# Three edits to a three-layer hybrid network on one core: SSD exponents on ScalarE, conditioning of the first layer by TensorE, gates stored as rows

## The chip, the cores and the metric

The kernel runs on one core of a Trainium2 chip. A core has five engines that run side by side, each with its own in-order instruction stream: TensorE (PE, with weight loads shown apart as PEld), VectorE (DVE), ScalarE (ACT), GpSimd (POOL) and SyncE (SP), which here issues every DMA. The metric is device time in microseconds, the median over several runs.

## The reference, cut to what matters

One block of a first kind (gated linear attention and a bidirectional SSD, both in chunks) is followed by two layers of a second kind. Every layer is conditioned: a vector c gives shifts, scales and gates. What the change touches is the conditioning and the SSD's decay between two tokens of a chunk.

```python
ada = jax.nn.silu(c)[:, None, :] @ w_ada[layer] + b_ada[layer]      # 1024 -> 6 x 1024
sh1, sc1, g1, sh2, sc2, g2 = jnp.split(ada, 6, axis=-1)
...
cum = jnp.cumsum(ai, axis=1)                                        # one SSD chunk of 128 tokens
seg = cum[:, :, None] - cum[:, None, :]
Lm = jnp.exp(jnp.where(mask, seg, -jnp.inf))
cb = jnp.einsum('btgn,bsgn->btsg', ci, bi)
y = jnp.einsum('btsg,btsge,bsgep->btgep', cb, Lm, xi)
y = y + jnp.einsum('btgn,bgenp->btgep', ci, S) * jnp.exp(cum)[..., None]
...
h_lat = h_lat + g1 * mix
h_lat = h_lat + g2 * _swiglu(modulate(rms_norm(h_lat, norm2_w[layer]), sh2, sc2), ...)
...
mod = cond @ w_ada[l] + b_ada[l]                                    # each of the two later layers
```

The sequence has 512 tokens and a context of 256, the model width is 1024. The SSD has 4 groups of 8 heads of width 64, in 4 chunks of 128 tokens, forward and backward.

## The kernel before, in words

Weights come in tiles of 128 x 1024 fp32. `feed` loads one (`wr`), ScalarE rounds it to a high part (`wh`), and DVE or POOL takes the rest (`wl`), so that each product is made of three fp32r matmuls (`mm3`). There are three buffers of each kind, so PE can run some tiles ahead of a late load, and no further.

The program is written as stages: start, `gla` (linear attention), `ssd`, the merge and the first layer's feed-forward, and then two layers of the second kind. A scheduler orders each engine's instructions by its own estimate of the times, with buffers and semaphores as limits, so neighbouring stages overlap. All DMAs are on SP's queue: one that waits for a free buffer holds back all that stand behind it.

In the `ssd` stage each group g goes through `ssd_dense` (the projections of B, C and x with a convolution, transposes through the PSUM bank `dtr`, of which there is one), `ssd_z` (a gate) and `ssd_scan`. For each chunk and each half of the heads, `ssd_scan` reads two broadcast rows of summed decays, `rf` and `rb` (three buffers each, 258 KB), takes from them the per-token columns of `TM` (one instruction on DVE, one on POOL), joins both by a predicated copy, takes the exponent on ScalarE and multiplies by `cb`. The result stands as weights before x on PE. At the end of a chunk, `a1` is divided by its norm (`ss`) on DVE, transposed and spilled to `sp_ob`.

Conditioning runs beside this, in 8 steps that `more(n)` pulls from `conditions()`: two for each of g1, sh2, sc2, g2 of the first layer. The later layers' vectors are pulled within the feed-forward stages. `cond_col` computes one vector: for each half of 512 columns it loads eight 128 x 512 pieces of the weight (`cw`), ScalarE scales each by an element of silu(c) per partition, POOL adds it to `cacc`; the sum is split into three bf16 parts (`rsc`, `qx`), and PE sums these over the partitions by products with one column of ones, twelve for each half. `to_row` then turns a gate into a row: the 128 x 8 tile is written to memory element by element (`rg1-1d`, `rg2-1d`, and `rg10d` to `rg21d` in the later layers), and read back much later as a row broadcast to all partitions (`row`).

The first two vectors (sh1, sc1) are made in the start stage in another way: the weight is a moving operand of 512 columns, silu(c) a stationary operand of 32 columns (`cs`), and four products fill the four strips of PE at once.

Of the kernel before, what the change touches and what calls it, by code (L numbers as in the profile page):

```python
# [7 lines left out]
F32 = mybir.dt.float32  # L8
# [37 lines left out]
def _col(v):  # L46

    return np.asarray(v).reshape(-1, P).T
# [19 lines left out]
def prep(x):  # L68
# [15 lines left out]
    w_ada = g["w_ada"][0]  # L84

    A["wa1"] = np.ascontiguousarray(w_ada[:, :2048].reshape(2, 4, P, 2, 4, 256).transpose(4, 0, 2, 1, 3, 5).reshape(4, 2, P, 2048))
    A["wa"] = np.ascontiguousarray(w_ada[:, 2048:])
    A["ba"] = np.ascontiguousarray(g["b_ada"][0][None, 2048:])
    lr = np.concatenate([cols("dtf"), cols("dtb"), cols("lrf"), cols("lrb"), np.zeros((D, 32), np.float32)], 1)
    A["w_lr"] = _feat(lr)[0]  # L90
    A["w_qk"] = np.stack([_feat(np.concatenate([cols("q", 128 * h, 128 * h + 128), cols("k", 128 * h, 128 * h + 128)], 1))
# [22 lines left out]
    pk = _Pack()  # L114
    c2 = np.stack([_col(g["c"][0]), _col(g["c_ctx"])], 2)
    pk.add("c2", c2.reshape(P, 16))
    ba = _col(g["b_ada"][0][:2048])
    pk.add("ba_sh", ba[:, :8])
    pk.add("ba_sc", ba[:, 8:])
    pk.add("gnw", _col(g["gla_norm_w"][0]))  # L120
    pk.add("snw", _col(g["ssm_norm_w"][0]))
    pk.add("n1w", _col(g["norm1_w"][0]))
# [91 lines left out]
def build(tc, I, out, at, dbg=None, stop=None):  # L214
# [71 lines left out]
    def PS(tag="sm"):  # L286
        return new(banks[-1].pool, [P, 512], F32, tag, banks[-1].tags[tag])
# [10 lines left out]
    def tt(o, a, b, op, e=V):  # L298
        note(o, e.tensor_tensor(o, a, b, op=op))  # L299

    def ts(o, a, s1, s2, op0, op1=None, e=V):
        if op1 is None:
            note(o, e.tensor_scalar(o, a, s1, None, op0=op0))  # L303
        else:
            note(o, e.tensor_scalar(o, a, s1, s2, op0=op0, op1=op1))
# [7 lines left out]
    def load(o, i):  # L313
        return note(o, nc.sync.dma_start(o, i))
# [110 lines left out]

    qp = es.enter_context(tc.tile_pool(name="qp", bufs=1))

    def cond_col(src, bias, cc, k0, plus, tag):

        r = qp.tile([P, NK], F32, name=tag)  # L430
        sums = []
        prev = recent[0]

        def late(i):
            tc.add_manual_dep(i.ins, prev, nosync, reason="not before")

        for j in range(2):
            acc = W("cacc", NC[0])
            late(memset(acc, 0.0))
            load(acc[0:1], bias[:, k0 + 512 * j:k0 + 512 * j + 512])  # L440
            for k in range(NK):
                w = W("cw", NC[1])
                late(load(w, src[k * P:(k + 1) * P, k0 + 512 * j:k0 + 512 * j + 512]))
                copy(w, w, scale=cc[k])
                tt(acc, acc, w, A_, e=G)

            s2, s3 = T([P, 2, 512], "rsc", 1, BF), T([P, 512], "qx", 1, BF)
            for i in range(2):
                copy(s2[:, i], acc)
                tt(s3 if i else acc, acc, s2[:, i], S_, e=G)  # L450
            sums.append([s2[:, 0], s2[:, 1], s3])
        yield None
        for j in range(2):
            p = PS("dtr" if "dtr" in banks[-1].tags else "o2")
            for k in range(4):
                for i, a in enumerate(sums[j]):
                    mm(p[:, k:k + 1], a[:, k * P:(k + 1) * P], ones_b[:, 0:1], i == 0, i == 2)
            ts(r[:, 4 * j:4 * j + 4], p[:, :4], plus, None, A_)
        yield r

    def silu_cols(src, tag):
        c1, th = qp.tile([P, NK], F32, name=tag), qp.tile([P, NK], F32, name=tag + "t")
# [4 lines left out]

    def to_row(c, scale, name):

        t = qp.tile([P, NK], F32, name=name)  # L470
        ts(t, c, scale, None, M_)
        d = dp.tile([NK, P], F32, name=name + "d")
        load(d.rearrange("k p -> p k"), t)
        return d.rearrange("k p -> (k p)")[None, :].to_broadcast([P, D])

    def row(d, tag, bufs=1):
# [7 lines left out]
        o, w = at[2][n]  # L484
        return Cl[l][:, o + a:o + (w if b is None else b)]

    cc = silu_cols(col("c2").rearrange("p (k j) -> p k j", j=2)[:, :, 0], "cc1")

    def conditions():

        for l, src, bias, n0, gs in ((-1, I["wa"], I["ba"], 2, 0.5), (0, I["w2a0"], I["b2a0"], 0, 1.0),
                                     (1, I["w2a1"], I["b2a1"], 0, 1.0)):
            for i, n in list(enumerate(("sh1", "sc1", "g1", "sh2", "sc2", "g2")))[n0:]:
                for r in cond_col(src, bias, cc if l < 0 else cc2, 1024 * (i - n0), 1.0 if n[:2] == "sc" else 0.0,
                                  f"m{n}{l}"):
                    if r is not None:
                        mod[l, n] = to_row(r, gs, f"r{n}{l}") if n[0] == "g" else r
                    yield

    mod = {}  # L500
    parts = conditions()
    NC = [2, 2]

    def more(n):
        for _ in range(n):
# [12 lines left out]
        t = T([P, S], "act", 25, F32R, ap)  # L518
        hC.append([t[:, :CTX], t[:, CTX:]])
    with phase("start"):  # L520
        cs = T([P, NK, 32], "cs")
        memset(cs, 0.0)
        th = T([P, 16], "th")
        act(th, col("c2"), AF.Tanh, scale=0.5)
# [330 lines left out]
    def ssd_steps():  # L855
# [4 lines left out]
        for n, o, nch in ((S, 0, 4), (CTX, S, 2)):  # L860
# [32 lines left out]
            if nch == 4:  # L893
                ts(Q, d3, 1e-37, None, OP.max)
                act(Q, Q, AF.Ln)
                tt(X[0:32], X[0:32], Q[0:32], S_)
                tt(X[32:64], X[32:64], Q[32:64], A_)
                copy(it[0:32], E1[0:32])
                copy(it[32:64], E2[32:64])
# [156 lines left out]
    def ssd_scan(g, d):  # L1056
# [24 lines left out]
        for c in range(4):  # L1081
# [3 lines left out]
            for hf in range(2):  # L1085
# [3 lines left out]
                for r_, rw in ((rf, fr), (rb, br)):  # L1089
                    load(r_, sp_A[rw, c * 129:(c + 1) * 129][None].to_broadcast([P, 4, 129]))  # L1090
                e1, e2 = rf[:, :, 1:129], rb[:, :, 0:128]
                tt(e1, e1, TM[:, c, 0, fr][:, :, None].to_broadcast([P, 4, P]), S_)
                tt(e2, TM[:, c, 0, br][:, :, None].to_broadcast([P, 4, P]), e2, S_, e=G)
                V.copy_predicated(e1, before, e2)
                act(e1, e1, AF.Exp)
                tt(e1, e1, cb[:, sl][:, None, :].to_broadcast([P, 4, P]), M_)
# [22 lines left out]
            act(sq, a1, AF.Square, acc=ss)  # L1119
            ts(ss, ss, 1.0 / 512, 4 * EPS, M_, A_)  # L1120
            rsq(ss)
            ts(a1, a1, ss, None, M_)
            ons.append(a1)
        for i in range(4):
            pt = PS()
# [4 lines left out]
    with phase("ssd"):  # L1130
# [8 lines left out]
            ssd_z(g, d)  # L1139
            ssd_scan(g, d)  # L1140
        more(8 - sum(MS))
        NC[:] = 2, 4
        for j in range(NG + NH, NK):
            gate_tile(I["w_gb"][j], sp_gb[j])
        oa = load_T(sp_oa)
# [766 lines left out]
```

## Time and profile before

| | |
|---|---|
| median of 3 runs | 2895.77 us (2894.13 to 2898.12) |
| profiled execution | 2891.66 us, of this the span 2889.7 us |
| granted TensorE clock, mean | 0.978 |
| PE, DVE, ACT, POOL busy | 94%, 64%, 46%, 40% of the span |
| conditioning weights, first layer (`cw<-in_wa`) | 64 DMAs of 256 KB |
| conditioning weights, later layers (`cw<-in_w2a`) | 192 DMAs of 256 KB |

Durations are of one profiled execution; the time of a run has some two microseconds outside its span. Matmuls overlap, so the sum of their durations is over the time they take; a pitch, from start to start, is the better number. A row of groups ends in the engine's idle time before them and what ended it. "Clock" is the share of TensorE's full clock that was granted in a window.

### The profile page before, as it was taken

Reading aid. Unit: us, or ns where it says so; the run is one execution under the profiler, and the core shown is the slowest. Engines: PE = TensorE matmul, PEld = TensorE weight load, DVE = VectorE, ACT = ScalarE, POOL = GpSimd, SP = SyncE. Lnnn points to the kernel's source line nnn. Section 1 sums busy time; section 2 is a strip of 40 time slices with the busy share of each in tenths; the row PEclk is TensorE's granted clock in tenths of the full one; section 3 lists DMA queues with packets and bytes.
Section 4 is the critical chain, followed back from the end, with each engine's and each line's share of the span. In section 5 each row is a group of like instructions: output and inputs, shape, how many; then the busy total and the mean of one; then the engine's idle time right before and its main releaser. Section 6 shows DMA issues by size and latency. Waiting matters only on the chain. (4 is left out here: it accounts for less than half of the span.)

```text
span 2889.7 us, 40511 instructions
## 1 busy us (share of the span) xinstructions
PE 2702.3 (94%) x15230; PEld 2215.4 (77%) x15230; DVE 1858.2 (64%) x2844; ACT 1328.7 (46%) x2307; POOL 1158.2 (40%) x790
## 2 busy tenths in 40 slices
PE   7999999988989899999999999999998999999997
PEld 5898988777776678777877877777777887788886
DVE  4777756968877475434555557764767655765457
ACT  5533334335343335634346654653634664443232
POOL 2333304536556144846631235574654123600013
PEclk9999999999999999999999999999999999999999
DMA  6222224444456754655422112655532220332222
GB/s 242 74 77 74 81 89 139 110 97 132 131 151 202 230 176 151 192 146 165 138 90 90 63 41 81 198 163 150 185 118 81 78 73 24 100 105 93 93 94 78
DMA packets 160308, 346.31 MB, mean 120 GB/s; under 512 B 20848, under 2 KB 55920, under 8 KB 159088
## 3 DMA queue, kind: packets, MB, share of 16 engines
q1 hardware_dynamic: 160112, 343.72, 38.6%
q8 instruction: 120, 1.97, 0.3%
q14 instruction: 76, 0.62, 0.1%
HBM read 326.73 MB, written 16.94 MB: 119 GB/s over the span
## 5 line engine op out<-in xcount | busy, mean ns | idle before, releaser
L311 PE MATMUL acc<-act,wh 128*128 128x512 f32 (+1 forms) x2944 | 877.5, 383 | 34.8 <-DVE act L299 16.9
L299 DVE TENSOR_TENSOR wl<-wr,wh 128x1024 fp32r<-128x1024 f32 (+1 forms) x329 | 466.9, 1421 | 442.6 <-ACT wh L296 441.8
L311 PEld LDWEIGHTS acc<-act,wh 128*128 128x128 f32 x2944 | 533.5, 193 | 161.0 <-DVE act L299 25.4
L296 ACT ACTIVATE wh<-wr 128x1024 fp32r<-128x1024 f32 (+1 forms) x344 | 358.9, 1045 | 510.2 <-PE sm L311 202.3
L311 PE MATMUL acc<-act,wl 128*128 128x512 f32 (+1 forms) x1472 | 530.6, 378 | 0.6 <-DVE wl L299 0.5
L311 PE MATMUL acc<-wh,act 128*128 128x256 f32 (+2 forms) x2312 | 499.7, 303 | 10.0 <-ACT cacc L290 7.1
L299 POOL TENSOR_TENSOR cacc<-cacc,cw 128x512 f32<-128x512 f32 x256 | 402.6, 1574 | 220.6 <-DMA cacc<-in_b2a_dram 86.4
L311 PEld LDWEIGHTS acc<-wh,act 128*128 128x128 f32 x2312 | 378.4, 190 | 31.2 <-ACT cacc L290 8.3
L311 PE MATMUL sm<-act,wh 128*128 128x512 f32 (+1 forms) x1232 | 376.2, 382 | 0.0
L311 PE MATMUL acc<-wl,act 128*128 128x256 f32 (+2 forms) x1156 | 350.5, 303 | 0.8 <-POOL wl L299 0.8
L311 PEld LDWEIGHTS acc<-act,wl 128*128 128x128 f32 x1472 | 273.0, 192 | 56.1 <-issue 8.2
L296 ACT ACTIVATE cw<-cw,cc 128x512 f32<-128x512 f32 x256 | 181.4, 721 | 262.0 <-DMA cw<-in_w2a_dram 155.3
L311 PEld LDWEIGHTS sm<-act,wh 128*128 128x128 f32 x1232 | 228.4, 189 | 46.3
L311 PE MATMUL sm<-act,wl 128*128 128x512 f32 (+1 forms) x616 | 235.0, 381 | 1.2 <-DVE wl L299 1.2
L311 PEld LDWEIGHTS acc<-wl,act 128*128 128x128 f32 x1156 | 220.0, 190 | 10.6 <-issue 1.9
L299 POOL TENSOR_TENSOR wl<-wr,wh 128x1024 fp32r<-128x1024 f32 x52 | 138.1, 2658 | 200.2 <-DVE wh L303 123.1
L299 POOL TENSOR_TENSOR wr<-wr,row 128x1024 f32<-128x1024 f32 x42 | 107.5, 2565 | 185.8 <-DMA f<-sp_yb 69.9
L299 POOL TENSOR_TENSOR x<-x,gx 128x512 f32<-128x512 f32 x32 | 49.4, 1570 | 300.0 <-DVE gx L299 300.0
L299 POOL TENSOR_TENSOR act<-act,wgt 128x128 f32<-128x128 f32 (+3 forms) x64 | 50.1, 801 | 246.3 <-DVE wgt L299 173.9
L311 PEld LDWEIGHTS sm<-act,wl 128*128 128x128 f32 x616 | 116.1, 189 | 25.7 <-DVE wl L299 2.5
L311 PE MATMUL sm<-wh,act 128*128 128x512 f32 (+1 forms) x392 | 124.2, 378 | 0.0
L1668 DVE CUSTOM_DVE_ANT_0 sm<-sm,K 128x128 f32<-128x128 f32 (+3 forms) x128 | 63.2, 497 | 86.1 <-PE sm L311 81.1
(440 smaller groups left out, 4626.1 us busy)
## 6 DMA issues: line engine op xcount, KB each, us to landing
cw<-in_w2a_dram SPq DMA_DIRECT2D x192, 256.0 KB
wr<-in_w2u_dram SPq DMA_DIRECT2D x88, 512.0 KB
wr<-in_w2d_dram SPq DMA_DIRECT2D x46, 512.0 KB
cw<-in_wa_dram SPq DMA_DIRECT2D x64, 256.0 KB
wr<-in_w_bcx_dram SPq DMA_DIRECT2D x24, 512.0 KB
wr<-in_w2ab_dram SPq DMA_DIRECT2D x24, 512.0 KB
wr<-in_w_dn_dram SPq DMA_DIRECT2D x23, 512.0 KB
wr<-in_w_g_dram SPq DMA_DIRECT2D x22, 512.0 KB
```

The source lines that it names most:

```text
L296: note(o, SC.activation(o, i, AF.Copy, scale=scale))
L299: note(o, e.tensor_tensor(o, a, b, op=op))
L311: return note(o, PE.matmul(o, l, r, start=st, stop=sp))
L1668: m = V.tensor_tensor_reduce(p[:, :n], p[:, :n], con2("NU")[:, S - n:], 1.0, 3e38, A_, OP.min, mx)
```

## The change

Four things are done.

First, `ssd_scan` forms both differences on ScalarE, head by head, as an identity with a bias per partition (`e2` with scale -1), so that 8 instructions of 128 columns take the place of one on DVE and one on POOL; the sign of `TM`'s first column block is turned for that (one swapped subtraction in `ssd_steps`). The scaling by the norm goes from DVE to ScalarE.

Second, the first layer's g1, sh2, sc2, g2 are made by PE in the form of the start stage, in 8 blocks of 512 columns (`cond_block`). The weight is laid out as 16 tiles of 1 MB in two buffers (`wa`), and `cond_loads` for the next block stands behind this block's products.

Third, a gate is stored as a row: in the first layer the 128 x 8 tile is transposed by PE, copied by ScalarE and written as eight rows of 128; in the later layers `cond_col` makes it as two rows of 512 at once, with ones as the stationary operand.

Fourth, the number of `cw` buffers (`NC`) is 4 from the start, where it was 2 up to the end of the scans; only later layers use them now.

```diff
-    A["wa"] = np.ascontiguousarray(w_ada[:, 2048:])
-    A["ba"] = np.ascontiguousarray(g["b_ada"][0][None, 2048:])
+    A["wa"] = np.ascontiguousarray(w_ada[:, 2048:].reshape(2, 4, P, 8, 512).transpose(3, 0, 2, 1, 4).reshape(8, 2, P, 2048))
...
+            if as_row:
+                for i, a in enumerate(sums[j]):
+                    mm(p[0:1], ones_b[:, 0:1], a, i == 0, i == 2)
+                t = new(qp, [1, 512], F32, "grow", 1)
+                copy(t, p[0:1])
+                load(d[:, 512 * j:512 * j + 512], t)
+                continue
...
     def to_row(c, scale, name):
-        t = qp.tile([P, NK], F32, name=name)
-        ts(t, c, scale, None, M_)
+        p = PS("dtr")
+        tr(p[:NK, :P], c)
+        t = new(qp, [NK, P], F32, "grow8", 1)
+        copy(t, p[:NK, :P], scale=scale)
         d = dp.tile([NK, P], F32, name=name + "d")
-        load(d.rearrange("k p -> p k"), t)
+        load(d, t)
...
-    cc = silu_cols(col("c2").rearrange("p (k j) -> p k j", j=2)[:, :, 0], "cc1")
+    cs = qp.tile([P, NK, 32], F32, name="cs")
+    def cond_loads(b):
+        prev, ws = recent[0], []
+        for hf in range(2):
+            ws.append(W("wa", 2, 2048))
+            tc.add_manual_dep(load(ws[hf], I["wa"][b, hf]).ins, prev, nosync, reason="not before")
+        return ws
+    def cond_block(r, b, ws):
+        pr = PS("dtr")
+        for hf, w in enumerate(ws):
+            for kk in range(4):
+                mm(pr[32 * kk:32 * kk + 32], cs[:, 4 * hf + kk], w[:, kk * 512:kk * 512 + 512], hf == 0, hf == 1)
+        t = W("ar")
+        copy(t, pr)
+        p = PS("dtr")
+        for i in range(4):
+            tr(p[:, i * P:(i + 1) * P], t[:, i * P:(i + 1) * P])
+        note(r, V.tensor_reduce(r, p.rearrange("p (i a j) -> p i j a", i=4, a=4)[:, :, 0], axis=mybir.AxisListType.X, op=A_))
+        stt(r, r, 1.0 if b in (4, 5) else 0.0, col("ba_r", 4 * b, 4 * b + 4), A_, A_)
     def conditions():
+        ws = cond_loads(0)
+        for i, n in enumerate(("g1", "sh2", "sc2", "g2")):
+            r = qp.tile([P, NK], F32, name=f"m{n}-1")
+            for j in range(2):
+                b = 2 * i + j
+                cond_block(r[:, 4 * j:4 * j + 4], b, ws)
+                if b < 7:
+                    ws = cond_loads(b + 1)
+                if j:
+                    mod[-1, n] = to_row(r, 0.5, f"r{n}-1") if n[0] == "g" else r
+                yield
...
-                tt(X[0:32], X[0:32], Q[0:32], S_)
+                tt(X[0:32], Q[0:32], X[0:32], S_)
...
-                tt(e1, e1, TM[:, c, 0, fr][:, :, None].to_broadcast([P, 4, P]), S_)
-                tt(e2, TM[:, c, 0, br][:, :, None].to_broadcast([P, 4, P]), e2, S_, e=G)
+                for h in range(4):
+                    act(e1[:, h], e1[:, h], AF.Identity, bias=TM[:, c, 0, fr][:, h:h + 1])
+                    act(e2[:, h], e2[:, h], AF.Identity, bias=TM[:, c, 0, br][:, h:h + 1], scale=-1.0)
...
-            ts(a1, a1, ss, None, M_)
+            act(a1, a1, AF.Identity, scale=ss)
```

The scheduler gives the engines new orders. Three places matter. On SP, while group 1 is scanned and group 2's z weights are due (`wr_6719`, `wr_6624`), the queue before the change holds the write of g1 (`rg1-1d`) ahead of the first weight pieces of sh2 (`cw`):

```order
L314 DMA rb_5990<-sp_A 128x4x129
L314 DMA rb_6003<-sp_A 128x4x129
L314 DMA wr_6719<-in_w_z_dram 128x1024
L314 DMA rg1-1d<-rg1-1_5475 128x8x1
L314 DMA cw_5483<-in_wa_dram 128x512
L314 DMA cw_5487<-in_wa_dram 128x512
L314 DMA rf_5946<-sp_A 128x4x129
L314 DMA rf_5989<-sp_A 128x4x129
L314 DMA cacc_5480<-in_ba_dram 1x512
L314 DMA cacc_5521<-in_ba_dram 1x512
L314 DMA cw_5491<-in_wa_dram 128x512
L314 DMA cw_5495<-in_wa_dram 128x512
```

and after it, with block 2's and then the eight rows of g1:

```order
L315 DMA rf_5831<-sp_A 128x4x129
L315 DMA rf_5880<-sp_A 128x4x129
L315 DMA rb_5949<-sp_A 128x4x129
L315 DMA wa_5452<-in_wa_dram 128x2048
L315 DMA wa_5454<-in_wa_dram 128x2048
L315 DMA rb_5968<-sp_A 128x4x129
L315 DMA rg1-1d<-grow_970_5458 8x128
L315 DMA rf_5899<-sp_A 128x4x129
L315 DMA wr_6624<-in_w_z_dram 128x1024
L315 DMA rf_5948<-sp_A 128x4x129
L315 DMA rb_6827<-sp_A 128x4x129
```

The write is now of 8 rows of 128, and the two 1 MB loads stand ahead of it; the sixteen `cw` pieces of a vector are four `wa` tiles.

On ACT, where group 1's first projections are evicted (`cv`, `bt`, `btc`, `cm`) while group 0 is scanned, before the change only the exponents of the scan (`rf<-rf`) stand between them:

```order
L296 ACTIVATE wh_5263<-wr_5261 128x1024
L290 ACTIVATE cv_5080<-acc_5055,cbh,cwh 128x512
L290 ACTIVATE rf_4786<-rf_4786 128x4x128
L290 ACTIVATE rf_4829<-rf_4829 128x4x128
L296 ACTIVATE bt_5037<-dtr_5038 128x512
L296 ACTIVATE btc_5044<-dtr_5045 128x256
L290 ACTIVATE cm_5085<-cv_5080 128x512
L290 ACTIVATE rf_4842<-rf_4842 128x4x128
L290 ACTIVATE sq_4767,ss_848_4766<-a_839_4743 128x512
L296 ACTIVATE wh_5345<-wr_5343 128x1024
```

and after it the differences stand there too, by fours on `rf` and `rb`, with the norm's scaling:

```order
L297 ACTIVATE wh_5250<-wr_5248 128x1024
L291 ACTIVATE cv_5067<-acc_5042,cbh,cwh 128x512
L297 ACTIVATE bt_5024<-dtr_5025 128x512
L291 ACTIVATE rb_4880<-rb_4880,TM 128x128
L291 ACTIVATE sq_4718,ss_832_4717<-a_823_4694 128x512
L291 ACTIVATE rb_4880<-rb_4880,TM 128x128 x3
L297 ACTIVATE btc_5031<-dtr_5032 128x256
L291 ACTIVATE rf_4811<-rf_4811,TM 128x128 x4
L291 ACTIVATE cm_5072<-cv_5067 128x512
L291 ACTIVATE a_823_4694<-a_823_4694,ss_832_4717 128x512
L291 ACTIVATE rf_4860<-rf_4860,TM 128x128 x4
L291 ACTIVATE rf_4811<-rf_4811 128x4x128
```

What stood there as two exponents is now a run of differences, with the scan's square (`sq`) and its scaling (`a_823`) between them; the copy `btc` and the eviction `cm` stand behind some of them.

On PE, in group 2's first projections beside group 1's scan, the sums of one vector before the change are one-column products on the bank `dtr`, between two runs of projections:

```order
L311 MATMUL acc_6159<-act_91,wh_6155 128x512
L311 MATMUL acc_6159<-act_92,wh_6155 128x512
L311 LDWEIGHTS rsc_4411
L311 MATMUL dtr_5447<-ones_b,rsc_4411 128x1
L311 LDWEIGHTS rsc_4411
L311 MATMUL dtr_5447<-ones_b,rsc_4411 128x1
L311 LDWEIGHTS qx_4412
L311 MATMUL dtr_5447<-ones_b,qx_4412 128x1
```

and after it a block is eight products with `wa` (the last four stand in the first row), followed by the scan's own, by projections, and ten rows later by the block's transposes (`ar`):

```order
L312 MATMUL dtr_5434<-wa_4395,cs 32x512 x4
L312 MATMUL sm_5743<-xh_5082,rf_5744 128x64 x4
L312 MATMUL sm_5743<-xh_5082,rf_5763 128x64 x4
L312 MATMUL sm_5784<-Sf_5412,cm_5072 128x512
L312 MATMUL acc_6130<-act_87,wl_6127 128x512
L312 MATMUL acc_6130<-act_89,wh_6126 128x512
L312 MATMUL acc_6130<-act_90,wh_6126 128x512
L312 MATMUL acc_6130<-act_89,wl_6127 128x512
L312 MATMUL acc_6130<-act_91,wh_6126 128x512
L312 MATMUL acc_6130<-act_92,wh_6126 128x512
L312 MATMUL acc_6130<-act_91,wl_6127 128x512
L350 MATMUL dtr_5445<-KC,ar_5443 128x128 x4
```

The same bank `dtr` takes both the block's products and its transposes.

More of the change, by code (lines that the diff above doesn't have):

```diff
@@ L116, in prep @@
     pk.add("c2", c2.reshape(P, 16))
-    ba = _col(g["b_ada"][0][:2048])
+    ba = _col(g["b_ada"][0])
     pk.add("ba_sh", ba[:, :8])
-    pk.add("ba_sc", ba[:, 8:])
+    pk.add("ba_sc", ba[:, 8:16])
+    pk.add("ba_r", ba[:, 16:])
     pk.add("gnw", _col(g["gla_norm_w"][0]))
@@ L426, in build, with cond_col @@
     qp = es.enter_context(tc.tile_pool(name="qp", bufs=1))
-    def cond_col(src, bias, cc, k0, plus, tag):
-        r = qp.tile([P, NK], F32, name=tag)
+    def cond_col(src, bias, cc, k0, plus, tag, as_row):
+        r = None if as_row else qp.tile([P, NK], F32, name=tag)
+        d = dp.tile([1, D], F32, name=tag + "d") if as_row else None
         sums = []
@@ L458, in cond_col @@
             ts(r[:, 4 * j:4 * j + 4], p[:, :4], plus, None, A_)
-        yield r
+        yield d.to_broadcast([P, D]) if as_row else r
     def silu_cols(src, tag):
@@ L485, in lcol @@
         return Cl[l][:, o + a:o + (w if b is None else b)]
-    cc = silu_cols(col("c2").rearrange("p (k j) -> p k j", j=2)[:, :, 0], "cc1")
-    def conditions():
[L491 to L495, printed above, removed]
+    cs = qp.tile([P, NK, 32], F32, name="cs")
@@ new lines, in conditions @@
+    def conditions():
+        ws = cond_loads(0)
[9 more added lines that the diff above has]
+                yield
+        for l in range(2):
+            for i, n in enumerate(("sh1", "sc1", "g1", "sh2", "sc2", "g2")):
+                for r in cond_col(I[f"w2a{l}"], I[f"b2a{l}"], cc2, 1024 * i, 1.0 if n[:2] == "sc" else 0.0, f"m{n}{l}",
+                                  n[0] == "g"):
@@ L496, in conditions @@
                     if r is not None:
-                        mod[l, n] = to_row(r, gs, f"r{n}{l}") if n[0] == "g" else r
+                        mod[l, n] = r
                     yield
@@ L501, in build @@
     parts = conditions()
-    NC = [2, 2]
+    NC = [2, 4]
     def more(n):
@@ L520, in build @@
     with phase("start"):
-        cs = T([P, NK, 32], "cs")
         memset(cs, 0.0)
@@ L1141, in build @@
         more(8 - sum(MS))
-        NC[:] = 2, 4
         for j in range(NG + NH, NK):
```

## The prediction

> **What bounds the kernel now.** I read the page first, then a table by stage, then who waits for whom in the stage that the change touches, then that stage's timeline.
>
> ```profile
> span 2889.7 us, 40511 instructions
> PE 2702.3 (94%) x15230; PEld 2215.4 (77%) x15230; DVE 1858.2 (64%) x2844; ACT 1328.7 (46%) x2307; POOL 1158.2 (40%) x790
> 430.00:1000.00 570.00, 508.37 (x2859) 412.80 (x2860) 420.10 (x576) 238.46 (x393) 281.69 (x216) 0.95 0.51 144
> 2528.22 8.40 PE acc L311 x36
> ```
>
> TensorE is the bound: 94% busy. Only its idle time (187 us) and its slow-clock time can be won. The third row is the SSD stage (columns: PE, weight load, DVE, ACT, POOL busy; clock; DMA share; GB/s): PE is idle for 570 - 508.4 = 61.6 us there, at a granted clock of 0.95, so another 0.05 x 570 = 28 us go to the clock. The last row, of the chain of waits, gives the full-clock pitch: 8.40 / 36 = 0.233 us for one 512-wide product.
>
> What PE waited for from 440 to 1000 us (total, times, longest):
>
> ```profile
> PE sm L311 <- DVE a L299: 14.7, 8, 3.9
> PE dtr L349 <- ACT bt L296: 9.6, 1, 9.6
> PE sm L311 <- DVE Sf L299: 8.5, 6, 2.8
> PE sm L349 <- DVE a L303: 5.4, 4, 2.2
> PE acc L311 <- ACT evd L296: 5.3, 1, 5.3
> PE sm L349 <- DVE a L299: 3.1, 4, 1.2
> PE dtr L349 <- ACT xh L296: 1.7, 2, 1.3
> ```
>
> The DVE lines, 14.7 + 8.5 + 5.4 + 3.1 = 31.7 us, are the scan waiting for a saturated VectorE. The ACT line is one wait of 9.6 us, and it is of another kind.
>
> **Term 1: the gates' element writes.** Six small DMAs write a gate to memory as 1024 elements of 4 bytes:
>
> ```profile
> L314 SPq DMA_DIRECT2D rg1-1d<-rg1-1_5475 x1: 360/360/360, 631.5 to 631.5; - x1
> L314 SPq DMA_DIRECT2D rg2-1d<-rg2-1_8297 x1: 383/383/383, 955.9 to 955.9; - x1
> L314 SPq DMA_DIRECT2D rg10d<-rg x1: 720/720/720, 1230.2 to 1230.2; - x1
> L314 SPq DMA_DIRECT2D rg20d<-rg x1: 378/378/378, 1426.7 to 1426.7; - x1
> L314 SPq DMA_DIRECT2D rg11d<-rg x1: 378/378/378, 1943.2 to 1943.2; - x1
> 634.00:643.00 9.00, 3.50 (x20) 2.79 (x19) 3.85 (x7) 0.00 (x0) 2.66 (x3) 0.89 0.53 28
> 647.00:652.00 5.00, 4.87 (x12) 2.94 (x13) 4.59 (x4) 1.48 (x4) 2.87 (x2) 0.57 0.27 84
> 1234.00:1243.00 9.00, 9.00 (x41) 7.40 (x40) 0.00 (x0) 0.00 (x0) 0.00 (x0) 1.00 0.64 28
> 1250.00:1256.00 6.00, 5.34 (x14) 4.24 (x15) 2.04 (x2) 3.15 (x5) 5.76 (x4) 0.55 0.82 247
> 1429.00:1438.00 9.00, 9.00 (x40) 7.29 (x39) 6.18 (x5) 2.94 (x4) 2.40 (x1) 1.00 0.21 20
> 1946.00:1955.00 9.00, 3.34 (x15) 2.38 (x13) 0.00 (x0) 0.00 (x0) 0.00 (x0) 0.82 0.59 23
> 1957.00:1962.00 5.00, 4.25 (x10) 3.35 (x11) 3.50 (x3) 5.00 (x7) 4.57 (x3) 0.50 0.56 161
> PE tp L311 <- ACT wh L296: 8.4, 1, 8.4
> PE tp L311 <- ACT wh L296: 2.8, 1, 2.8
> PE tp L311 <- DVE wl L299: 1.3, 1, 1.3
> 981.82 0.63 ACT L296 ACTIVATE act<-evl 128x512 fp32r<-128x512 f32 x1 [5.13 <-DMA evl<-sp_ob]
> ```
>
> For about nine microseconds after each write the DMA engines are up to 0.64 busy and move 20 to 28 GB/s, where the stage has 144. A conditioning weight queued behind the write lands late, ScalarE stands in order before it, the weight casts behind ScalarE wait, and PE runs dry; then it restarts at half clock. Prices: 631: 9.6 us idle plus 5 x 0.43 = 2.1 of clock, 11.7. 1230: 2.8 + 1.3 idle plus 6 x 0.45 = 2.7, 6.8. 1943: 8.4 plus 5 x 0.50 = 2.5, 10.9. 1427: PE stayed at 9.00 of 9, nothing; the sixth, in the second layer's up-projection, I take to be like it. 956: the 5.3 us (ACT evd) end 26 us later, behind a load of the scan's last output (last row), and would partly stand without it; I count 3.6. Together 33. Bounds: the idle of the three sure ones, 9.6 + 4.1 + 8.4 = 22, and all of 956 with its clock, 42. Eight rows of 512 B or two of 2 KB replace 1024 pieces; I take them to leave no hole. The transposes and copies that make the rows (two of 128 columns for layer one; 24 products of 512 columns in place of 96 of one column for the gates of layers two and three) are 24 x 0.233 = 5.6 us against 8.3 (the row for the same count below): nothing. Eight more ScalarE copies lie under its 54% idle.
>
> **Term 2: decay exponents and row norm off DVE and POOL.**
>
> ```profile
> L299 DVE TENSOR_TENSOR rf<-rf,TM 128x512 f32<-128x512 f32 x32 | 30.7, 963 | 15.0 <-DMA rf<-sp_A 15.0
> L303 DVE TENSOR_SCALAR a<-a,ss 128x512 f32<-128x512 f32 x16 | 17.3, 1079 | 4.4 <-POOL ss L299 4.2
> L299 POOL TENSOR_TENSOR rb<-TM,rb 128x512 f32<-128x512 f32 x32 | 41.1, 1285 | 65.1 <-DMA rb<-sp_A 57.2 <-DVE wl L299 7.3 <-DVE rf L299 0.6
> L299 POOL TENSOR_TENSOR cacc<-cacc,cw 128x512 f32<-128x512 f32 x64 | 93.5, 1461 | 59.6 <-DMA cacc<-in_ba_dram 37.5 <-ACT cw L296 21.7
> L296 ACT ACTIVATE cw<-cw,cc 128x512 f32<-128x512 f32 x64 | 46.0, 721 | 101.6 <-DMA cw<-in_wa_dram 98.0 <-POOL wd L299 1.8 <-POOL cacc L299 1.4
> L290 ACT ACTIVATE act<-act,wgt 128x128 f32<-128x128 f32 x16 | 5.5, 392 | 2.8 <-DVE wgt L299 2.8
> ```
>
> DVE loses 30.7 + 17.3 = 48 of its 420 us, POOL 41.1 + 93.5 = 134.6 of 282. Where PE waited, DVE had no room:
>
> ```profile
> 520.00:530.00 10.00, 7.14 (x41) 5.67 (x42) 10.00 (x13) 2.90 (x5) 5.97 (x6) 0.92 0.46 140
> 660.00:670.00 10.00, 8.31 (x45) 6.65 (x44) 10.00 (x14) 2.06 (x5) 8.49 (x7) 1.00 0.55 159
> 680.00:690.00 10.00, 8.15 (x38) 6.10 (x38) 10.00 (x13) 5.91 (x10) 10.00 (x8) 0.94 0.45 127
> ```
>
> The DVE waits fall, not by all: I take 22 of 31.7 plus what their clock costs. Bounds: 0 (ScalarE becomes as late) and 47 (all 31.7 and half of the 28 us of clock). ScalarE gains 256 pieces of 128 columns at 5.5 / 16 = 0.344 us (overlapped), 88 us, and 16 of 512 columns, about 11; it loses the 46.0 of the weight scaling and 10 of splitting the sums. Net +43, to 281 of 570. It must also now stand before the rf and rb loads (15.0 + 57.2 us of waits on DVE and POOL), with the weight casts queued behind it and PE behind those; against that its 98.0 us of waits for conditioning weights go. I take the waits as even.
>
> The Trainium skill ("ScalarE: Activation LUTs", Rules for kernel authors) says to put add and mul on VectorE, not ScalarE. By that rule the move loses: 99 us on ScalarE against 48 on DVE, and with that difference of +51 in place of -22 the sum would be -33 + 51 + 21.5 = +39.5, 2935. The row for 430 to 1000 speaks against the rule here: 420.1 of 570 busy on DVE, 238.5 on ScalarE.
>
> **Term 3: conditioning on PE.**
>
> ```profile
> 37.06 1.06 PE L311 MATMUL dtr<-wa,cs 128*32 128x512 f32 x8
> 41.66 0.60 PE L349 MATMUL sm<-KC,ar 128*128 128x128 f32 x4
> L311 PE MATMUL dtr<-ones_b,rsc 128*128 128x1 bf16 x64 | 5.0, 165 | 0.0
> L311 PE MATMUL dtr<-ones_b,qx 128*128 128x1 bf16 x32 | 3.3, 165 | 0.0
> ```
>
> The start stage already works in this form: a half block is 1.06 us (four strips at once), the transposes 0.60. Eight blocks cost 8 x (2 x 1.06 + 0.60) = 21.8; the 96 one-column products, 8.3, go. +13.5; bounds 0 (all in PE's idle) and 27 (all at half clock).
>
> **Term 4: late loads.** A load waits on SP for the block before it to leave PE, with rf, rb and w_z loads queued behind it. Blocks 2, 4, 6 and 7 follow close on their predecessors in PE's order: between 1 and 2 lie 26 products of 512 and 6 of 256 columns, 26 x 0.233 + 6 x 0.117 = 6.8 us, and the scan's own. One MB takes 7 us at the stage's 144 GB/s. I take 1 us for each, +4; bounds 0 and 14 (a second half 3.5 late each time).
>
> **Term 5: one dtr bank.** Product, ScalarE copy, transposes and DVE sum of a block pass through the only dtr bank, between the transposes of x, B and C. Sixteen hand-overs; the nearest row, PE's two waits for ACT xh on the same bank, has 1.3 at most. +4; bounds 0 and 16.
>
> Nothing: the removed start-up silu and 32 more columns in C lie under PE's wait for its first weights; the swapped subtraction has the same count.
>
> **Sum.** -33 - 22 + 13.5 + 4 + 4 = -33.5. The profiled execution is 2891.66 us (span 2889.7), so 2858; the median of the runs is 4.1 us above it, so **2862**.
>
> **Rivals.** (a) Only the rows pay: term 2 is 0, since the exponents leave a DVE queue for a ScalarE queue with DMA waits. -33 + 21.5 = -11.5: 2884. For it: ScalarE is in order and feeds every weight. Against: DVE was full (10.00 of 10) in the three stretches of term 2, ScalarE at most 5.91. (b) ScalarE becomes the bound of the scans: its net 43 us lie wholly on the path. -33 + 21.5 + 43 = +31.5: 2927, slower. It decides once ScalarE's work and waits in a scan exceed PE's; at 281 of 570 it is far from that on average. This is what the rule about VectorE would do here. (c) The holes are not due to the writes' pieces and remain: -22 + 21.5: 2895, no change. Against: the hole follows the write in all four places shown. The Trainium skill ("DMA: Bandwidth & Descriptors", Specifications) says that transfers under 512 B are read, modified and written; the trace agrees in that 4-byte pieces go with 20 to 28 GB/s, but shows no row of 512 B. (d) More: -42 - 47 + 13.5 = -75.5: 2820.
>
> **Chances.** My sum 0.54, (a) 0.20, (b) 0.06, (c) 0.08, (d) 0.12. Faster by over 0.2% (5.8 us, about what can be told from no change): 0.54 + 0.20 + 0.12 = 0.86; the same 0.08; slower 0.06. The range reaches from half way to (d), 2836, past (a), to 2888.
>
> **What would show it.** No stretch of nine microseconds under 30 GB/s with DMA engines busy; no single PE wait over 6 us from 600 to 2000. The SSD stage's DVE under 380 us and PE's DVE waits near 12. ScalarE near 280 there; were it above 330, or the casts to wh late, (b) is at work. PE's waits for wa near 4. I am wrong above all if ScalarE's waits for rf and rb hold up the casts, or if the new order opens waits elsewhere.

## The result, and the profile after

The changed kernel takes 2831.53 us (median of 4 runs, 2826.53 to 2835.49), the kernel before 2894.95 beside it: a ratio of 0.978 (95% interval 0.9761 to 0.9798). It is faster by 63 us, where 34 were forecast, and lies 4.5 us under the low end of the range. The profiled execution took 2826.53 us, the quickest of the four. One run of `p2_after_128` below, the profiled one, took 3770 us at a granted clock of 0.66 and is left out, so that its time is the median of its four other runs and its products are not counted.

The head of the page, after:

```profile
span 2824.8 us, 40315 instructions
PE 2688.7 (95%) x15224; PEld 2216.3 (78%) x15224; DVE 1791.2 (63%) x2780; ACT 1370.1 (49%) x2516; POOL 1006.7 (36%) x678
```

PE's total hardly moves (2702.3 before): what went is idle time, and, as will be seen, a little of the time of each product. Where in the program it went is read from a landmark, the first load of the weight `w_out` just behind the SSD stage. The two rows are from the view of one tensor's instructions, before and after; the numbers behind the durations are the first and last issue.

```profile
L314 SPq DMA_DIRECT2D wr<-in_w_out_dram x9: 327/333/383, 1009.5 to 1053.1; - x9
```

```profile
L315 SPq DMA_DIRECT2D wr<-in_w_out_dram x9: 328/332/382, 967.8 to 1010.4; - x9
```

Up to there 41.7 us were won, behind it (2889.7 - 1009.5 = 1880.2 before, 2824.8 - 967.8 = 1857.0 after) 23.2. By the terms of the prediction it was to be 11.7 + 3.6 + 22 - 21.5 = 15.8 up to there and 17.7 behind. So most of the miss lies up to there, with the SSD stage. Its row in the table by stage (PE, weight load, DVE, ACT, POOL busy; clock; DMA share; GB/s), before and after, for the same 530 us:

```profile
430.00:960.00 530.00, 475.89 (x2733) 387.64 (x2734) 409.15 (x563) 226.13 (x376) 281.69 (x216) 0.95 0.50 140
```

```profile
430.00:960.00 530.00, 512.51 (x2943) 414.67 (x2944) 355.68 (x526) 277.49 (x595) 128.49 (x104) 0.98 0.51 156
```

PE's idle time fell from 54.1 to 17.5 us and its clock rose by 0.03. DVE lost 53 us of work, more than the 48 that were taken off it, although it did more of the scans in these 530 us; POOL lost more than half. What PE still waited for from 440 to 960 us, after (total, times, longest):

```profile
PE sm L312 <- DVE rf L300: 4.0, 2, 2.7
PE acc L312 <- DVE cv L309: 2.9, 2, 2.3
PE dtr L312 <- DVE cm L309: 1.7, 1, 1.7
PE acc L312 <- DVE ss L306: 1.6, 1, 1.6
PE acc L312 <- ACT evd L297: 1.4, 1, 1.4
PE dtr L312 <- DMA wa<-in_wa_dram: 1.2, 1, 1.2
PE sm L312 <- DVE a L300: 0.9, 2, 0.7
PE dtr L350 <- ACT xc L297: 0.5, 1, 0.5
PE dtr L350 <- ACT bt L297: 0.4, 1, 0.4
```

The 31.7 us of waits for DVE's `a` and `Sf` are down to 0.9. With those for `rf`, `cv`, `cm` and `ss`, some of them new, PE's waits for DVE are 11.1 us in all, near the 12 that the prediction named. The nine microseconds behind the gates' writes, after, in the order g1 and g2 of layer one, then g1 and g2 of layer two and g1 of layer three:

```profile
632.00:641.00 9.00, 9.00 (x51) 6.02 (x50) 7.50 (x11) 7.56 (x22) 3.57 (x4) 1.00 0.47 135
896.00:905.00 9.00, 9.00 (x45) 7.44 (x44) 3.19 (x4) 3.94 (x6) 0.00 (x0) 1.00 0.64 212
1190.00:1199.00 9.00, 9.00 (x40) 7.27 (x39) 2.08 (x3) 4.20 (x6) 3.89 (x4) 1.00 0.62 205
1370.00:1379.00 9.00, 9.00 (x41) 7.46 (x40) 1.83 (x3) 1.74 (x3) 0.00 (x0) 1.00 0.39 118
1898.00:1907.00 9.00, 9.00 (x41) 7.48 (x40) 5.84 (x3) 6.02 (x8) 6.54 (x4) 1.00 0.73 233
```

118 to 233 GB/s where 20 to 28 went behind four of these writes before, and PE is busy throughout; behind the sixth it is 71, where it was 27. One thing more is only seen where PE waits for nothing. Hundred microseconds near the end, before and after:

```profile
2600.00:2700.00 100.00, 100.00 (x430) 80.51 (x429) 46.58 (x56) 29.54 (x35) 0.00 (x0) 1.00 0.28 91
```

```profile
2600.00:2700.00 100.00, 100.00 (x441) 82.38 (x440) 51.94 (x64) 29.32 (x36) 0.00 (x0) 1.00 0.30 99
```

At 100% busy and a full clock PE starts 441 products in place of 430: 0.227 us for one, not 0.233. The change edits nothing in these products.

### The profile page after: what moved, and what is told of

Same layout as the page of the kernel before. It is cut to its first block, busy times and chain, and to the rows that moved or that the text cites. A ratio compares the mean times of both kernels' runs of the same rounds, so it can differ in the third digit from the quotient of the medians.

```text
span 2824.8 us, 40315 instructions
## 1 busy us (share of the span) xinstructions
PE 2688.7 (95%) x15224; PEld 2216.3 (78%) x15224; DVE 1791.2 (63%) x2780; ACT 1370.1 (49%) x2516; POOL 1006.7 (36%) x678
## 4 chain that ended last, share of the span: by engine, by line
PE 69%; DVE 9%; ACT 6%; DMA 6%; POOL 6%; issue 3%; SPq 0%; DVEq 0%; POOLq 0%; ACTq 0%
PE acc L312 36%; PE sm L312 18%; PE o L312 6%; POOL cacc L300 4%; PE ab L312 3%; DMA cw<-in_w2a_dram 2%; PE tp L312 2%; DVE wl L300 2%; PE sm L350 1%; POOL x L300 1%; PE dtr L312 1%; ACT wh L297 1%; DVE act L300 1%; PE tp L350 1%; DMA rf<-sp_A 1%
## 5 line engine op out<-in xcount | busy, mean ns | idle before, releaser
L300 DVE TENSOR_TENSOR wl<-wr,wh 128x1024 fp32r<-128x1024 f32 (+1 forms) x329 | 459.0, 1397 | 419.3 <-ACT wh L297 414.8
L300 POOL TENSOR_TENSOR cacc<-cacc,cw 128x512 f32<-128x512 f32 x192 | 312.4, 1629 | 139.6 <-DMA cacc<-in_b2a_dram 82.5
L297 ACT ACTIVATE cw<-cw,cc 128x512 f32<-128x512 f32 x192 | 135.9, 721 | 141.5 <-DMA cw<-in_w2a_dram 136.7
```

The costliest lines, as they stand in the source:

```text
L297: note(o, SC.activation(o, i, AF.Copy, scale=scale))
```

## The experiments

The change has three parts that can be had one by one: R, the gates as rows; E, exponents and norm on ScalarE; B, the block form of the first layer's conditioning on PE (with the number of `cw` buffers, which then only later layers use). "Before" in a comparison is the kernel before on the same chip in the same session.

### One part alone

Kernel `e1_rows`: the kernel before with R.

```diff
-        load(d.rearrange("k p -> p k"), t)
+        tr(p[:NK, :P], c)
+        copy(t, p[:NK, :P], scale=scale)
+        load(d, t)
...                                        # and cond_col's as_row for the later layers, as in the change
```

> Against the kernel before, only the six gate writes are rows. The prediction's price is -33 us (bounds -22 and -42). Theory A (the forecast's price of the exponents was too small, those of the rows and of the block form are right): -33. Theory B (the block form, priced at +21.5, is really free or a gain, because it takes 64 small loads, the weight scaling and the accumulation off the other engines): -33 as well. Theory C (the rows are worth more than the holes showed): under -42. Rival (c) of the prediction: 0, and stretches of nine microseconds under 30 GB/s remain after the writes.

Kernel `e2_exp`: the kernel before with E.

```diff
-                tt(e1, e1, TM[:, c, 0, fr]...)
-                tt(e2, TM[:, c, 0, br]..., e2, S_, e=G)
+                    act(e1[:, h], e1[:, h], AF.Identity, bias=...)
+                    act(e2[:, h], e2[:, h], AF.Identity, bias=..., scale=-1.0)
-            ts(a1, a1, ss, None, M_)
+            act(a1, a1, AF.Identity, scale=ss)
```

> Against the kernel before, only the decay exponents and the norm's scaling are on ScalarE; the weight scaling of the first layer's conditioning stays there too. The prediction's price is -22 us (0 to -47). Theory A: -47 or more, and PE's waits for DVE (a, Sf) in the scans nearly gone. Theory B: -22 to 0, since ScalarE and POOL still carry the conditioning. Rival (b), ScalarE as the bound: slower than before.

Kernel `e3_cond`: the kernel before with B, the gates written as elements.

```diff
-                for r in cond_col(src, bias, cc if l < 0 else cc2, ...)
+                cond_block(r[:, 4 * j:4 * j + 4], b, ws)
+                    ws = cond_loads(b + 1)
```

> Against the kernel before, only the first layer's conditioning is in blocks on PE, with the gates still written as elements. The prediction's price is +21.5 us (terms 3 to 5; 0 to +57). Theory A: +15 to +25. Theory B: -5 or less, with ScalarE's waits for conditioning weights and POOL's accumulation gone and DVE's operations shorter.

Measured against 2892.83: R 2867.27 (-25.6; ratio 0.991, 0.9898 to 0.9923), E 2888.91 (-3.9; 0.9974 to 0.9993), B 2885.40 (-7.4; 0.9968 to 0.9987). The sum is -37, not -63. R is a quarter under its price, E is almost nothing, and B, priced at +21.5, is a gain. Theory A falls with E (3.9 where it had 47), theory C and rival (c) with R. Theory B has the ranges of E and B right, and R a quarter too large; but the sum leaves 26 us that the parts only have together.

### Two parts together, and the norm

Each of these is the changed kernel with one part put back; the edits are those above in reverse, and in `e7_norm_back` only the last line of E's.

> The changed kernel (2831.5) with the six gates written as elements again, so block form and exponents together. Alone the three parts gave -26, -4 and -7, sum -37, while together they give -61 to -63. Theory D (exponents and block form need each other: the block form frees ScalarE and POOL, the exponents then free DVE): this pair is worth -35 to -40 of before, so about 2856. Theory E (the rows need one of the others: with a hole in the load queue the freed engines have nothing to do): this pair is worth about its parts, -11, so 2880 or more.

> The changed kernel with the exponents and the norm's scaling back on DVE and POOL, so rows and block form. Theory D: the sum of the parts, -33, so 2860. Theory E: -45 or more, 2848 or less.

> The changed kernel with the old conditioning of the first layer (64 loads, ScalarE scaling, POOL sums), so rows and exponents. Theory D: the sum of the parts, -30, so 2863. Theory E: -45 or more, 2848 or less. The prediction's terms, taken by themselves: -55.

> The changed kernel with only the norm's scaling (16 instructions of 128x512) back on DVE; the exponents stay on ScalarE. By the prediction's term 2, where DVE loses 30.7 + 17.3 us, this part would be worth a third, some 7 us: 2838. If the scans are no longer bound by DVE in the changed kernel: within 3 us of it, 2829 to 2834.

Measured against 2893.82:

| kernel | parts | us | less than before | ratio, 95% |
|---|---|---|---|---|
| `e4_no_rows` | E B | 2865.23 | 28.6 | 0.9884 to 0.9916 |
| `e5_no_exp` | R B | 2844.60 | 49.2 | 0.9816 to 0.9842 |
| `e6_no_cond` | R E | 2865.30 | 28.5 | 0.9893 to 0.9919 |
| `e7_norm_back` | R B, exponents | 2838.00 | 55.8 | 0.9794 to 0.9819 |

E and B need each other, but not all of 35 to 40 (theory D): together 28.6, where their parts make 11. R and B together have 16 more than their sum, which theory D did not foresee; theory E did, but fails on the two other pairs. R and E have 2.9 more than R alone, within what can be told. The norm is worth 6.5 us by the times (2838.00 - 2831.53), 7.6 by each kernel's own before, where some 7 were priced. In the hundred microseconds of full PE, `e5_no_exp` and `e7_norm_back` had the short pitch (442 and 441 products), the other kernels of this and the last section the long one (430 or 431). So the pitch comes with R and B together, where neither part touches these products.

### Where the tiles lie

R and B both change a few small tiles that are allocated ahead of the activations; so the activations move against the weight tiles (`wr`, `wh`, `wl`, which lie at one address modulo 256; B moves these too). The difference of the addresses of the first activation and the first `wh`, modulo 256 bytes, is 128 before, 64 with R, 128 with E, 64 with B, E B or R E, and 0 with R B and in the changed kernel. Neither address decides by itself: modulo 256 the activations lie at 96 both in the kernel before (430 products) and in the changed one (441), and the weights at 224 both in the kernel before and in two of those below that have 441. Four kernels whose instructions stand on each engine as in the kernel they are made from, but with unused bytes (32 floats here, 64 and 48 in others):

```diff
-    qp = es.enter_context(tc.tile_pool(name="qp", bufs=1))
+    qp = es.enter_context(tc.tile_pool(name="qp", bufs=1)); qp.tile([P, 32], F32, name="pad")
```

> The kernel before with 128 unused bytes put ahead of the pool qp; every engine's instructions stand as before, only the activations and all that lies behind them move by 128 bytes against the weight tiles. Seen so far: where PE never waits and the granted clock is 1.00, the kernels with both rows and block form start 439 to 442 products in 100 us, all others 430 to 431. Theory P (the place of the tiles sets PE's pitch: it is the short one where the activations' address minus the weights' is a multiple of 256 bytes, as in the three quick kernels and in none of the others): this kernel has the short pitch, and about 24 us less than before, 2869. Theory Q (the pitch comes from the order of the programs or from another part of the change): no change, within 6 us of 2893, and 430 products in 100 us.

> The changed kernel with the same 128 unused bytes; the program is the same. Theory P: the long pitch returns, 430 products in 100 us near the end, and about 24 us more than the changed kernel, 2856. Theory Q: within 6 us of 2831.

> The changed kernel with 256 unused bytes, a control. Theory P: the difference of the addresses is again a multiple of 256, so the short pitch stays and the time with it, within 6 us of 2831. If any shift of the tiles lengthens the pitch, or if the rule is another (a multiple of 512, or the address itself): 2845 to 2860. Theory Q: within 6 us of 2831, as for 128 bytes.

> The kernel with rows alone (26 us under before) and 192 unused bytes, which make the difference of the addresses a multiple of 256 there. Theory P: the short pitch, about 24 us less, so some 50 us under before, 2843. Theory Q: no change, 26 us under before, 2867.

Measured against 2892.91: the kernel before with 128 bytes 2876.46 (-16.4; 0.993 to 0.9955); the changed kernel with 128 bytes 2844.44 (0.9821 to 0.9847) and with 256 bytes 2831.86 (0.9772 to 0.9807), so 12.6 apart; rows with 192 bytes 2854.10, 13.2 more than rows without had won against its own before. By the times theory P holds on all four, with 13 to 16 us in place of the 24 expected; Q falls. The same hundred microseconds of the kernel before with 128 bytes, the changed kernel with 256 and the rows with 192:

```profile
2600.00:2700.00 100.00, 100.00 (x441) 82.48 (x440) 49.90 (x61) 27.95 (x33) 0.00 (x0) 1.00 0.28 95
2600.00:2700.00 100.00, 100.00 (x441) 82.38 (x440) 51.93 (x64) 29.32 (x36) 0.00 (x0) 1.00 0.29 99
2600.00:2700.00 100.00, 100.00 (x441) 82.52 (x440) 47.24 (x57) 27.76 (x32) 0.00 (x0) 1.00 0.27 95
```

and the landmark of the first:

```profile
L314 SPq DMA_DIRECT2D wr<-in_w_out_dram x9: 328/333/382, 1010.7 to 1054.7; - x9
```

All three have 441 products. In the first and the third the weights lie where they do in the kernel before, at 224 modulo 256. The first kernel comes to `w_out` no sooner than before (1009.5): up to there, with the SSD stage in which PE waits, a shorter product gives nothing. Its 13.2 us of span (2889.7 to 2876.5) are all behind it, and nearly all of them late: the first load of `w2d` is issued at 1905.1, where it was 1906.5.

### Why the block form is a gain

Without the tiles' part the change is worth 48.5 us (2892.91 to 2844.44), still 15.0 over the forecast. What the block form takes away or adds was put back by itself, in the changed kernel, in eighths behind each block:

```diff
+                    note(pd, G.tensor_tensor(pd, pd, pd, op=M_))          # s1: x64, POOL
+                    note(pd, SC.activation(pd, pd, AF.Copy, scale=1.0))   # s2: x64, ScalarE
-        for hf, w in enumerate(ws):
+        for hf, w in list(enumerate(ws)) * 2:                             # s3: PE's products twice
```

and in the kernel with rows and exponents alone, for the waits of the old form:

```diff
-    NC = [2, 2]
+    NC = [2, 8]                                                           # s6
```

> The changed kernel with 64 idle products of 128x512 on POOL added, eight behind each conditioning block, as much as the sums of the old form cost there (93.5 us); no loads and no ScalarE work come with them. Theory L (the block form pays by POOL's relief: POOL's work makes DVE's longer, and holds up the scan's own POOL steps): DVE's time from 430 to 960 us grows by 15 to 25 us, and the kernel by 10 to 20, to 2842 to 2852. Theory M (it pays because ScalarE no longer stands in order before 64 small loads, 98.0 us of waits before): within 4 us of 2831.

> The changed kernel with 64 idle copies of 128x512 on ScalarE added, eight behind each block, as much as the weight scaling of the old form (46 us), without its waits for loads. Theory L and theory M: within 5 us of 2831. Theory N (ScalarE's plain work was the price, since it feeds every weight): 10 us more or over.

> The changed kernel with the products of each block done twice, 8 x 2 x 1.06 = 17 us more on PE by the prediction's price, and nothing else. If the added work stands on the path, as term 3 had it: +13 to +17, 2845 to 2849. If it falls into idle time of PE: within 5 us of 2831; PE is idle for only 17.5 us from 430 to 960 in the changed kernel, so I lean to the first.

> The kernel with rows and exponents and the old conditioning (2865.3), with eight buffers for its small weight pieces in place of two, so that loads run ahead and ScalarE need not wait for them. Theory M: ScalarE's waits for these pieces fall under 10 us (37.2 there) and the kernel gains 10 us or more, 2855 or less. Theory L: within 5 us of 2865, since POOL's sums stay.

On this chip the kernel before took 2903.55, 10 more than on the others, and the changed kernel was not run there; so the first three are compared among themselves. POOL 2846.37, ScalarE 2828.48, PE twice 2832.98. POOL's work costs 13 to 18 us over the other two, and 17 us more on PE cost 4.5 against ScalarE's kernel, where I had leaned to 13 or more. ScalarE's 46 us show no cost: the changed kernel took 2831.53 and 2830.35 elsewhere. With eight `cw` buffers 2871.66, 31.9 under its before where two had 28.5, and by the time 6.4 over the two; the intervals of the ratios (0.9873 to 0.9902, 0.9893 to 0.9919) overlap. ScalarE's waits for `cw` fell only from 37.2 to 17.1 us, so that M is tested by half, but there is no sign of its 10 us. Theory L holds in the time; DVE's time from 430 to 960 us grew by 13.9 us (355.7 to 369.6), a little less than its 15 to 25. PE's waits from 440 to 960 us are 25.4 us with POOL's products, 14.6 in the changed kernel; those for DVE grew by 7.3, and those for `wa` by 4.0, for which no run here has the reason. The two largest with POOL's products (total, times, longest):

```profile
PE acc L312 <- DVE cv L309: 6.9, 3, 4.5
PE dtr L312 <- DMA wa<-in_wa_dram: 5.2, 2, 3.0
```

How POOL's work lengthens DVE's is seen in DVE's groups from 430 to 960 us. The changed kernel:

```profile
L300 DVE TENSOR_TENSOR a<-sm,TM 128x512 f32<-128x512 f32 x32 | 21.7, 682 | 2.6 <-PE sm L312 2.6
L300 DVE TENSOR_TENSOR a<-a,sz 128x512 f32<-128x512 f32 x16 | 10.9, 681 | 0.1
L309 DVE SCALAR_TENSOR_TENSOR own<-TM,cbd,dsk 128x8 f32<-128x8 f32 x16 | 4.9, 314 | 0.0
```

With POOL's 64 products:

```profile
L300 DVE TENSOR_TENSOR a<-sm,TM 128x512 f32<-128x512 f32 x32 | 21.7, 679 | 6.1 <-PE sm L312 6.1
L300 DVE TENSOR_TENSOR a<-a,sz 128x512 f32<-128x512 f32 x16 | 13.0, 813 | 0.1
L309 DVE SCALAR_TENSOR_TENSOR own<-TM,cbd,dsk 128x8 f32<-128x8 f32 x16 | 7.7, 484 | 0.1
```

and before:

```profile
L299 DVE TENSOR_TENSOR a<-sm,TM 128x512 f32<-128x512 f32 x32 | 21.7, 677 | 1.2 <-PE sm L311 1.2
L299 DVE TENSOR_TENSOR a<-a,sz 128x512 f32<-128x512 f32 x16 | 12.6, 786 | 0.0
L308 DVE SCALAR_TENSOR_TENSOR own<-TM,cbd,dsk 128x8 f32<-128x8 f32 x16 | 14.3, 901 | 1.9 <-POOL a L299 1.9
```

An instruction that reads one operand from PSUM (`sm`) takes 680 ns in all three. Those that read two from SBUF are longer with POOL's work: `own` 484 and 901 ns where it was 314, `a<-a,sz` 813 and 786 where it was 681. The Trainium skill ("SBUF — State Buffer", Who interferes with whom) says that a DVE instruction with two SBUF inputs contends with a GpSimd instruction that reads SBUF, and one with at most one does not, unless it runs in a mode that uses both of DVE's port pairs. The trace agrees for these three groups; the norm's `a<-a,ss`, with one tensor from SBUF, took 1079 ns before and 713 with rows and block form, and in which mode it ran is not shown. So a product on POOL for which nobody waits can still cost DVE time. Between the kernels with R and with R and B, whose DVE work differs only by the old form's small steps, DVE's time from 430 to 960 us falls from 412.6 to 386.7:

```profile
430.00:960.00 530.00, 484.62 (x2798) 393.87 (x2796) 412.63 (x564) 231.77 (x387) 283.34 (x216) 0.97 0.49 147
```

```profile
430.00:960.00 530.00, 501.97 (x2862) 400.42 (x2860) 386.66 (x564) 187.89 (x315) 173.44 (x136) 0.97 0.49 147
```

### POOL's difference, and the pieces of the writes

Kernel `s4_rb_pool`: the changed kernel with `e2`'s difference on POOL again. Kernel `s5_pieces`: with one write more behind each gate's rows. `a2_after_again`: the changed kernel, beside both.

```diff
-                    act(e2[:, h], e2[:, h], AF.Identity, bias=..., scale=-1.0)
+                tt(e2, TM[:, c, 0, br]..., e2, S_, e=G)                   # s4
+            i = load(d.rearrange("k p -> p k"), pd[:, :, 0])              # s5: 1024 pieces of 4 bytes
+            i = load(d, pd[:, 0, :8])                                     #     128 of 32
+            i = load(d.rearrange("k p c -> p k c"), pd)                   #     1024 of 64
```

> The changed kernel with the backward difference (rb, 32 instructions, 41 us) back on POOL; the forward one stays on ScalarE. Both exponents and the norm are worth 13 us there, the norm alone 6.5, so 6.5 are left for rf and rb. By the 64 added POOL products (83.5 us of work, some 15 us of time, 0.18 for one) rb's 41 us are worth 7. If the exponents act through POOL: 5 to 8 us more than the changed kernel. If they act through DVE (rf): within 2 us of it.

> The changed kernel with one idle write more behind each gate's rows, of three kinds in turn: 1024 pieces of 4 bytes (behind g1 of layer 1 and g2 of layer 2), 128 pieces of 32 bytes (g2 of layer 1, g1 of layer 3), 1024 pieces of 64 bytes (g1 of layer 2, g2 of layer 3). If the hole goes by the number of pieces: both 1024-piece kinds leave some nine microseconds under 30 GB/s and take as long from issue to landing, and 128 pieces take about an eighth of it and leave none. If it goes by bytes: 4 KB in 128 pieces is as slow as in 1024, and 64 KB takes many times longer. The time: 5 to 20 us over the changed kernel.

> The changed kernel again, as the measure for the other two on the same chip: 2831, 0.978 of before.

Measured: 2831.89, 2837.25 and 2830.35, before 2894.23. The changed kernel repeats (0.978, 0.9766 to 0.9795). With `rb` on POOL again it is 1.5 slower, within what can be told: POOL's time is not worth the same everywhere, and here 40 us came off ScalarE in return (235.7 busy from 430 to 960, for 277.5). My 7 us for it fall, and of E's 14 us beside R and B the norm has 6.5; the rest is DVE's difference or not to be told apart by these runs.

The pieces, in rows of `s5_pieces`: 4 bytes (two writes), 32 bytes (two), and 64 bytes (the first) while they were written:

```profile
632.00:640.00 8.00, 6.99 (x36) 4.26 (x34) 2.66 (x5) 1.83 (x7) 0.00 (x0) 1.00 0.40 30
1383.00:1392.00 9.00, 9.00 (x41) 7.47 (x40) 2.50 (x3) 2.40 (x3) 0.00 (x0) 1.00 0.23 27
905.00:913.00 8.00, 8.00 (x40) 6.57 (x40) 3.30 (x4) 3.16 (x5) 0.00 (x0) 1.00 0.80 247
1908.00:1916.00 8.00, 8.00 (x37) 6.59 (x37) 3.99 (x3) 5.41 (x7) 3.87 (x2) 1.00 0.68 222
1201.00:1203.00 2.00, 2.00 (x10) 1.64 (x9) 1.48 (x3) 0.00 (x0) 0.00 (x0) 1.00 0.92 167
```

Each write of 4-byte pieces brings back the hole, 27 to 30 GB/s for eight or nine microseconds; the same 4 KB in 128 pieces leave none; and 1024 pieces of 64 bytes, sixteen times the bytes, were through within two microseconds (their packets lie from 1201.1 to 1202.4 us). Neither of the two expected rules holds: the same count of larger pieces is quick, and so are the same bytes in fewer pieces. It takes many pieces of 4 bytes; why, and from which size on 1024 pieces are quick, no run here shows. The time is 6.9 over the changed kernel's, within the 5 to 20 expected.

## Why the prediction was wrong, point by point

The direction was right. Along one chain of kernels the 63.4 us are: rows 25.6, the block form behind them 23.6 (of which the tiles' place has 13 to 16), exponents and norm last 14.2.

- **The largest failed step is terms 3 to 5 (+21.5): they had the wrong sign.** Beside rows the block form gains 8 to 11 us of its own (23.6 less the tiles' part), alone 7.4; that is some 30 us from the forecast. Term 3 charged PE's added work in full; twice the products cost 4.5 us, not 17. Terms 4 and 5 charged 8 us for late loads and the one bank; PE waited 1.2 us for `wa`, and 1.7 + 0.5 + 0.4 = 2.6 for DVE and ScalarE on `dtr` (`cm`, `xc`, `bt`). And the sentence on DVE and POOL counted POOL's 93.5 us as POOL's alone: the relief was worth 13 to 18 us, in good part through DVE's instructions, and I priced it at nothing.
- **The other failed step is a missing term.** "Only its idle time (187 us) and its slow-clock time can be won" left out the pitch of a busy PE. The change moves tiles, and with them the pitch of its products, 0.233 to 0.227 us, where PE is full. I took the pitch from the trace of before and used it for the kernel after. This is 13 to 16 us. Nothing in the trace of before showed it; the experiments of the unused bytes do.
- **Luck.** The changed kernel without the tiles' part, 2844.44, lies inside the range, but only because terms 1 and 2 were 7.4 and 7.8 us too large and so hid half of the error in terms 3 to 5.
- **Term 2 (-22) was right only with the block form beside it.** Alone 3.9, beside rows 2.9 (28.5 - 25.6), beside the block form 21.2 (28.6 - 7.4), beside both 14.2. It came near its bound of 0 without the block form, but not for the reason given, that ScalarE might become as late: in the changed kernel ScalarE stood at 277.5 of 530 us, and 46 us more showed no cost; with rows and exponents PE still waited 17.2 us for DVE's `a`.
- **Term 1 (-33) was the right mechanism, priced a third to a half too high.** Rows alone gave 25.6, and 22.4 with the short pitch on both sides (2876.46 to 2854.10). The holes up to `w_out`, priced at 15.3, gave 18.6, and those behind it, priced at 17.7, gave 8: with the short pitch on both sides `w_out` comes at 1010.7 without rows and at 992.1 with them (first row below), and from there to the end are 2876.5 - 1010.7 = 1865.8 and 2849.9 - 992.1 = 1857.8 us. With the long pitch on both sides (second row, `e1_rows`, span 2865.5 us) it is 22.4 and only 1.8. These are single executions, and a load marks PE's place only roughly; both pairs show that the holes behind `w_out` were priced too high, but not why:

```profile
L315 SPq DMA_DIRECT2D wr<-in_w_out_dram x9: 328/332/382, 992.1 to 1035.9; - x9
L315 SPq DMA_DIRECT2D wr<-in_w_out_dram x9: 327/332/381, 987.1 to 1031.3; - x9
```

- **Rivals.** (a), that the exponents pay nothing, would have been nearly right without the block form (rows and exponents: 28.5, rows 25.6). (b) did not appear, and neither did what the rule on VectorE would have made of it. The Trainium skill ("Perfetto Trace Analysis", Optimizing Scalar/DVE Operations) says in turn that where DVE is saturated, moving some work to ScalarE may make sense; the trace agrees, with DVE's 10.00 of 10 in three stretches before and 14.2 us won beside the other parts. (c) fell: the holes went and came with the 4-byte pieces. The 20 to 28 GB/s named with it are all that the engines moved then, not the pace of the pieces: 4 KB in nine microseconds are 0.46 GB/s. (d) has the time best, with a wrong reason for part of it.
- **What was to show it.** No stretch under 30 GB/s behind the six writes; the longest wait of PE from 600 to 2000 us was 4.9 (row below); PE's waits for DVE at 11.1, for `wa` at 1.2; ScalarE at 277.5 of 530 us, and its waits for `rf` and `rb`, 39.1 us, held up no cast that PE waited for there. DVE has 355.7 of 530 us; over the 570 us that the prediction read it has 385.7, just over the 380 named, but there the changed kernel is already past the stage. So nearly all came out on the good side, and none of them could have shown the pitch: I had named no row in which PE does not wait.

```profile
PE sm L350 <- ACT gx L291: 7.8, 3, 4.9
```

- **Slips.** Half way from 2862 to (d) at 2820 is 2841, not 2836, and term 2's upper bound is 31.7 + 14 = 45.7, not 47. Neither changes the argument.

## What to carry to other kernels

Work on an engine with much idle time isn't free if it reads from SBUF beside a full DVE: before a step on POOL is priced at nothing, compare DVE's instructions with two SBUF inputs to those fed from PSUM. Count products in a stretch where PE never waits, before and after: if their number moves and the program's products do not, it is the place of the tiles, and a few unused bytes tell. A part whose engine is relieved by another part should be priced beside it, not alone.

## What the runs showed of the hardware that I had not expected

PE's pitch depends on where activations and weights lie against each other: with a difference that is a multiple of 256 bytes 441 products of 512 columns start in 100 us, with 64 or 128 bytes more 430 to 431, at the same granted clock of 1.00. The Trainium skill ("SBUF — State Buffer", Who interferes with whom) says that PE has two independent read ports, one for the moving operand and one for the weights, and never waits on anyone; by that the place should not matter, and the measured difference is 2.5%. What causes it no run here shows, and whether another difference (192 bytes, say) is as good or better was not tried.

A piece of 4 bytes is a case of its own: 1024 of them take the queue some nine microseconds, 1024 of 64 bytes less than two. The prediction cited the Trainium skill ("DMA: Bandwidth & Descriptors", Specifications) for transfers under 512 bytes as a class; in these runs 128 pieces of 32 bytes and 1024 of 64 left no hole, and only the 1024 of 4 bytes did.
